# Seven products for eight in the up-projections of three feed-forward layers

## The chip, the core and the metric

The kernel runs on one core of a Trainium2 chip. The metric is the device time of one execution in microseconds (us), lower is better. Engines are named as in the profile: PE (TensorE, matrix products), DVE (VectorE), ACT (ScalarE), POOL (GpSimd), SP (here only an issuer of transfers).

## What is computed

Two blocks act on 512 tokens of 1024 features in float32. The first has two layers, each a mixer (a gated linear recurrence, then a sparse attention) and a convolutional feed-forward layer; the second has a gated feed-forward layer, a hybrid mixer and another gated feed-forward layer. The change is in the last three feed-forward layers: the convolutional one behind the attention, and both of the second block.

```
def swiglu(x, w_gu, w_down):                 # D_FF = 2816
    g, u = jnp.split(x @ w_gu, 2, axis=-1)   # w_gu [1024, 5632]
    return (jax.nn.silu(g) * u) @ w_down     # w_down [2816, 1024]

def conv_ffn(h, w_up, conv_w, conv_b, w_down):
    a, v = jnp.split(h @ w_up, 2, axis=-1)
    a = causal_conv3(a, conv_w) + conv_b     # along the tokens, per feature
    return (jax.nn.silu(a) * v) @ w_down
```

## The kernel before, in words

The residual `x` stays in SBUF, features on partitions. Every float32 operand of a large product is split into two float32r parts, h = round(a) on ACT (L186, L315) and l = a - h on DVE (L187, L318), and a product is three matmuls: h h, h l and l h (`fm`, L249, lines L274, L275, L277; `tm`, L284, with tokens on the output's partitions). Each matmul has a 128x128 weight tile of its own and up to 512 tokens.

All weights pass through one stream in the order of use. A block is 1024 rows (8 k tiles) by 256 columns; `w_dma` (L161) loads it on SP's queue into one of two raw buffers, `w_split` (L172) splits it in eight chunks of 512 elements per partition into one of three buffers for h and l, and `w_done` (L206) lets the next one start when a block has been used.

A feed-forward layer (`ffn`, L926) goes in three rounds, of 3, 4 and 4 groups. A group is 256 features: a block of the gate's columns and one of the value's columns, 96 matmuls of 512 tokens (the first group of a layer goes by token halves, 256 tokens, since its input is still being normalised). Gate tiles leave PSUM through `ev_a` (L937; silu, with the convolution also L950 and L952), value tiles through `ev_v` (L965; product L968 on DVE, then a split into the down projection's operand, L315 and L318). Then the round's part of the down projection is added to `x` (`out_proj`, L639; `resid`, L621, with L632); the last round's goes by token halves in its second half, and each half starts the next norm (`norm_half`, L394, with L376 and L388 or L390, and L428 where two norms follow each other). Squares for the norm are added up on POOL (L337).

The program order of each engine is the order in which the builder emits instructions. `Weave` (L64) counts the time of emitted matmuls, 0.000424 us per column, and lets side tasks (splits, norms, parts of mixers) emit their next step when their delay on that clock is over; `wait` runs a task to its end at once. PSUM has four banks for products (`pg`, L142) and four for side tasks (`pa`, L146).

Of the kernel before, what the change touches and what calls it, by code (L numbers as in the profile page):

```python
# [16 lines left out]
OP = mybir.AluOpType  # L17
# [10 lines left out]
RAW_BUFS, HL_BUFS, W2_BUFS = 2, 3, 10  # L28
# [24 lines left out]
class Tiles:  # L53
    """a [128, k, token] tile, with other tiles in place of its first ones."""
# [9 lines left out]
class Weave:  # L64
    """Interleaves side generators with the main stream, by emitted tensor-engine time (us)."""
# [13 lines left out]
    def _run(self, task):  # L79
        """one step; a generator yields the time to its next step, or None while it is blocked."""  # L80
        self.busy = True
        blocked = False
        try:
            dt = next(task.gen)
            blocked = dt is None
            self.n += 1
            heapq.heappush(self.q, (self.t + (0.3 if blocked else dt), self.n, task))
        except StopIteration:
            task.done = True
        self.busy = False  # L90
        return blocked
# [7 lines left out]
    def wait(self, task):  # L99
        """runs the task to its end, and others only while it is blocked."""  # L100
# [17 lines left out]
class Builder:  # L118
    def __init__(self, tc, I, out, ctx):
# [8 lines left out]
        self.nm = 0  # L128

# [21 lines left out]
    def w_init(self, blocks):  # L151
        self.wb = blocks
        self.w_dma_i = self.w_split_i = self.w_use_i = self.w_done_i = 0
        self.w_raw = {}
        self.w_hl = {}
        self.w_task = {}
        self.w_hold = False
        self.w_held = []
        self.gain = None

    def w_dma(self):  # L161
        i = self.w_dma_i
        if i >= len(self.wb):
            return
        self.w_dma_i += 1
        ap, r0, nk, c0, ncol = self.wb[i]
        raw = self.t([128, nk, ncol], "raw", RAW_BUFS)
        src = ap[r0 * 128:(r0 + nk) * 128, c0:c0 + ncol].rearrange("(k p) m -> p k m", p=128)
        self.nc.sync.dma_start(raw, src)
        self.w_raw[i] = raw  # L170

    def w_split(self, i, slow=True):  # L172
        nc = self.nc
        if i >= len(self.wb):
            return
        while i != self.w_split_i:
            yield None
        _, _, nk, _, ncol = self.wb[i]
        raw = self.w_raw.pop(i)
        h = self.t([128, nk, ncol], "wh", HL_BUFS, F32R)  # L180
        l = self.t([128, nk, ncol], "wl", HL_BUFS, F32R)
        self.w_hl[i] = (h, l)
        step = max(1, 512 // ncol)
        for k in range(0, nk, step):
            e = min(nk, k + step)
            nc.scalar.activation(h[:, k:e], raw[:, k:e], AF.Copy)  # L186
            nc.vector.tensor_tensor(l[:, k:e], raw[:, k:e], h[:, k:e].bitcast(F32), op=OP.subtract)  # L187
            if slow:
                yield MISC_D[0]
        self.w_split_i += 1  # L190
        self.w_dma()

    def w_start(self):
        self.w_dma()
        self.w_dma()
        for i in range(HL_BUFS):
            self.w_task[i] = self.wv.spawn(self.w_split(i), W2_D if i == 2 else 0.0)

    def w_get(self, want):
        i = self.w_use_i  # L200
        assert self.wb[i][1:] == want[1:] and str(self.wb[i][0]) == str(want[0]), (self.wb[i], want)
        self.w_use_i += 1
        self.wv.wait(self.w_task.pop(i))
        return self.w_hl.pop(i)

    def w_done(self, delay=0.7):  # L206
        i = self.w_done_i + HL_BUFS
        self.w_done_i += 1
        if i < len(self.wb):
            if self.w_hold:  # L210
                self.w_held.append(i)
            else:
                self.w_task[i] = self.wv.spawn(self.w_split(i), delay)
# [15 lines left out]
    def fm_merged(self, X, jobs, k_wait=None):  # L229
        """as fm, but with all of the jobs' features side by side in one loop over k; k_wait: (k, task) has  # L230
        the tiles from k on written by the task."""
# [4 lines left out]
        for k in range(nk):  # L236
            if k_wait is not None and k == k_wait[0]:
                self.wv.wait(k_wait[1])
            for j, m, p in todo:
                h, l = got[j]  # L240
                c = slice(m * 128, m * 128 + 128)
                self.mm3(p, h[:, k, c], l[:, k, c], xh[:, k, :], xl[:, k, :], k == 0, k == nk - 1)
# [3 lines left out]
        for _ in jobs:  # L246
            self.w_done()

    def fm(self, X, jobs, halves=False, kint=False, waits=(), last_delay=0.7):  # L249
        """jobs: list of (block, evac(mt_in_block, ps, lo, hi)); out[feature, token]."""  # L250
# [4 lines left out]
        for i, (lo, hi) in enumerate(parts):  # L255
# [3 lines left out]
            for jb, (b, ev) in enumerate(jobs):  # L259
                if jb not in got:  # L260
                    got[jb] = self.w_get(b)
                h, l = got[jb]
# [3 lines left out]
                for grp in groups:  # L266
                    pss = [self.pg() for _ in grp]
                    late = LATE if halves and kint and jb == 0 else 0
                    for k in range(nk + late):
                        for (m, mw), p in zip(grp, pss):  # L270
                            c = slice(m * 128, m * 128 + mw)
                            j = k - late
                            if k < nk:
                                mm(p[:mw, :n], h[:, k, c], xh[:, k, lo:hi], start=k == 0, stop=False)  # L274
                                mm(p[:mw, :n], l[:, k, c], xh[:, k, lo:hi], start=False, stop=False)  # L275
                            if j >= 0:
                                mm(p[:mw, :n], h[:, j, c], xl[:, j, lo:hi], start=False, stop=j == nk - 1)  # L277
# [3 lines left out]
                if i == len(parts) - 1:  # L281
                    self.w_done(last_delay if jb == len(jobs) - 1 else 0.7)

    def tm(self, X, jobs, halves=False, waits=()):  # L284
        """jobs: list of (block, evac(tok_tile, ps)); out[token, feature]."""
# [6 lines left out]
        for i, (j, t) in enumerate(order):  # L292
# [5 lines left out]
            h, l = got[j]  # L298
            nk, n = b[2], b[4]
            p = self.pg()  # L300
            for k in range(nk):
                tk = slice(t * 128, t * 128 + 128)
                mm = self.nc.tensor.matmul
                mm(p[:, :n], xh[:, k, tk], h[:, k, :], start=k == 0, stop=False)  # L304
                mm(p[:, :n], xh[:, k, tk], l[:, k, :], start=False, stop=False)  # L305
                mm(p[:, :n], xl[:, k, tk], h[:, k, :], start=False, stop=k == nk - 1)  # L306
                self.wv.pe(3 * n * 0.000424)
            ev(t, p)
            if t == 3:
                self.w_done()  # L310

    def split(self, h, l, src, engine="act"):
        """h + l = src, h and l float32r."""
# [7 lines left out]
    def norm_new(self, double=None):  # L321
        """squares of tiles below NPE are added up, the others go to the tensor engine one by one."""
# [24 lines left out]
    def rstd(self, ps, lo, hi):  # L347
        """[token, tile] reciprocal root of mean square + eps, from sums over 1024."""
# [8 lines left out]
    def bcast(self, ps, r, lo, hi):  # L357
        """ps[:, token] = r[token] on every partition."""
# [5 lines left out]
    def norm_outs(self, X, lo, hi, steps, ks=range(KT)):  # L364
        """X[k] = x[k] * gs[k] * ps (+ sh[k]) as float32r halves; steps(k): (gs, ps, sh)."""
# [28 lines left out]
    def norm_half(self, X, lo, hi, gs, sh=None, prev=None):  # L394
# [8 lines left out]
        if self.n_double is not None:  # L403
            # the second norm's mean square is the sum of (x g)^2 times the first's rstd^2
# [39 lines left out]
    def params(self):  # L444
        """Vectors over features, as columns: rows of 128 features are loaded and transposed."""
# [70 lines left out]
    def ada_cols(self, layer, j, acc, pai):  # L516
        """columns j*4 .. j*4+3 of the modulation, from partial sums over partitions."""
# [30 lines left out]
    def ada_first_load(self, js):  # L548
        """shift and scale of the first norm: 2048 columns, as four blocks in the big slots."""
# [7 lines left out]
    def ada_first_sums(self, j, pool=0):  # L557
        """sums over a block's row tiles, the first of them on the scalar engine and Pool."""
# [8 lines left out]
    def ada_first_mm(self, j):  # L567
        """a block's columns, as products on the tensor engine, each 128 times over."""
# [38 lines left out]
    def gs(self, name, layer, which):  # L607
        """norm gain times (1 + scale)."""
# [5 lines left out]
    def gs_part(self, t, name, layer, which, k0):  # L614
        """as gs, for four tiles of features."""
# [5 lines left out]
    def resid(self, first_mt, scale, norm):  # L621
        """evacuator: x[mt] += scale * ps."""
# [42 lines left out]
    def norm_to(self, gs, sh=None, double=None, tags=("hTh", "hTl")):  # L665
        """for out_proj's last blocks: a norm into a fresh X."""
# [8 lines left out]
    def next_norm(self, gs, sh=None, tags=("hTh", "hTl")):  # L675
        """starts a norm whose halves run as side tasks; returns (X, after_half)."""
# [9 lines left out]
    def hg_masks(self):  # L686
        """mask[m][s, t]: s in the first, t in the second half of the same block of 2m; mask[0]: s == t."""
# [23 lines left out]
    def hg_core(self, pair, v, o, B, done, gated, gain):  # L711
        """two heads: o[head] = rms-normed output of the gated recurrence, without its gain."""
# [62 lines left out]
        # s["T"]: [128, 4] chunk decays; q and k now carry the decay from and to the chunk's ends  # L775
# [140 lines left out]
    ROUNDS = ((0, 6), (6, 14), (14, 22))  # L916

    def ffn_blocks(self, up, down):
        out = []
        for a, b in self.ROUNDS:  # L920
            for t in range(a, b, 2):
                out += [(up, 0, 8, t * 128, 256), (up, 0, 8, DFF + t * 128, 256)]
# [3 lines left out]
    def ffn(self, X, waits, up, down, scale, after, conv=None):  # L926
        """x += scale * (act(X up_a) * (X up_v)) down; act: silu, or silu of the causal convolution."""
        nc = self.nc
        if conv is not None:
            cw, cb = conv  # L930
        for r, (a, b) in enumerate(self.ROUNDS):
            mh, ml = self.big("b0", F32R), self.big("b1", F32R)
            for t in range(a, b, 2):
# [36 lines left out]
                first = r == 0 and t == a  # L970
# [950 lines left out]
```

## Time and profile before

| | us |
|---|---|
| median of 3 runs (lowest, highest) | 2780.48 (2775.51, 2782.68) |
| span of the profiled execution, first to last instruction | 2771.8 |
| median less span | 8.7 |
| PE busy / PE weight loads busy | 2725.3 / 2309.7 |
| DVE busy / ACT busy / POOL busy | 1466.6 / 1052.3 / 280.1 |
| mean granted PE clock | 0.995 |

The page lists the span, and for the profiled execution no time of its own beside it. Matmuls overlap in the pipeline, so one matmul's duration is longer than the distance to the next, and a PE that is always busy can still be slow: what a stage takes is read from the distances. "Busy" of another engine includes time in which a started instruction is held up.

### The profile page before, as it was taken

The page shows a single profiled execution, that of the slowest core. Times are in us where ns is not written, and L with a number is a line of the kernel's source. Part 1 is how long each engine was busy: PE and PEld are TensorE (multiplying, and loading weights), DVE is VectorE, ACT ScalarE, POOL GpSimd, SP SyncE. Part 2 cuts the span into 40 slices and gives each one's busy share as a digit, 9 for nine tenths or more (in the row PEclk, how much of TensorE's full clock was granted, in tenths as well). Part 3 has the DMA queues.
Part 4 walks back from the last instruction along what each step waited for, and adds up shares of the span by engine and source line. Part 5 has one row for each costly group of instructions (what it writes and reads, how often), then busy time and mean ns, then how long its engine had stood idle before and what let it go on. Part 6 is the DMA issues. An engine that isn't in the chain of part 4 may idle for free.

```text
span 2771.8 us, 36529 instructions
## 1 busy us (share of the span) xinstructions
PE 2725.3 (98%) x14561; PEld 2309.7 (83%) x14561; DVE 1466.6 (53%) x2791; ACT 1052.3 (38%) x2044; POOL 280.1 (10%) x404
## 2 busy tenths in 40 slices
PE   6999999999999999999999999999999999999999
PEld 5988898888978888888889888897878987988888
DVE  7866567767544896544446333353455235533333
ACT  3323343323323895433334232343256333422222
POOL 3111110000101792000011000010000000100001
PEclk9999999999999999999999999999999999999999
DMA  7542126555231001233222322323433233232221
GB/s 251 185 152 71 59 92 198 175 175 182 79 107 61 1 2 64 97 100 106 91 92 84 99 91 97 102 63 108 105 78 88 54 89 105 77 101 96 92 92 60
DMA packets 254183, 278.69 MB, mean 101 GB/s; under 512 B 12952, under 2 KB 228397, under 8 KB 254013
## 3 DMA queue, kind: packets, MB, share of 16 engines
q1 hardware_dynamic: 226283, 233.21, 27.0%
q10 hardware_dynamic: 27730, 43.14, 4.8%
q8 instruction: 115, 1.88, 0.3%
q14 instruction: 55, 0.45, 0.1%
HBM read 274.23 MB, written 2.10 MB: 100 GB/s over the span
## 4 chain that ended last, share of the span: by engine, by line
PE 92%; DVE 4%; ACT 1%; POOL 1%; issue 1%; ACTq 0%; DMA 0%; DVEq 0%; POOLq 0%
PE pg L274 26%; PE pg L275 26%; PE pg L277 26%; PE pa L733 2%; PE pg L306 1%; PE pg L304 1%; PE pg L305 1%; PE pa L1279 1%; DVE w L546 1%; PE pa L1322 1%; PE pa L360 1%; PE pg L1238 1%; PE pg L1237 1%; PE pa L1048 1%; PE pa L344 1%
## 5 line engine op out<-in xcount | busy, mean ns | idle before, releaser
L187 DVE TENSOR_TENSOR wl<-raw,wh 128x512 fp32r<-128x512 f32 x842 | 571.1, 711 | 426.6 <-ACT wh L186 425.0
L274 PE MATMUL pg<-b,wh 128*128 128x512 f32 (+1 forms) x1856 | 672.6, 363 | 1.0 <-DVE w L968 1.0
L275 PE MATMUL pg<-b,wl 128*128 128x512 f32 (+1 forms) x1856 | 667.2, 360 | 0.0
L274 PE MATMUL pg<-hTh,wh 128*128 128x512 f32 (+3 forms) x1672 | 638.4, 383 | 1.8 <-ACT hTh L315 1.2
L275 PE MATMUL pg<-hTh,wl 128*128 128x512 f32 (+3 forms) x1672 | 633.1, 380 | 0.7 <-DVE wl L187 0.7
L277 PE MATMUL pg<-hTl,wh 128*128 128x512 f32 (+3 forms) x1672 | 621.5, 376 | 0.0
L186 ACT ACTIVATE wh<-raw 128x512 fp32r<-128x512 f32 x842 | 477.6, 619 | 279.8 <-PE pg L277 173.4
L277 PE MATMUL pg<-b,wh 128*128 128x512 f32 (+1 forms) x1472 | 523.9, 358 | 0.0
L275 PEld LDWEIGHTS pg<-b,wl 128*128 128x128 f32 x1856 | 348.8, 188 | 56.4
L274 PEld LDWEIGHTS pg<-b,wh 128*128 128x128 f32 x1856 | 348.6, 188 | 56.5 <-DVE w L968 1.4
L274 PEld LDWEIGHTS pg<-hTh,wh 128*128 128x128 f32 (+2 forms) x1672 | 313.4, 187 | 72.5 <-issue 4.6
L277 PEld LDWEIGHTS pg<-hTl,wh 128*128 128x128 f32 (+2 forms) x1672 | 310.4, 188 | 66.8 <-DVE hTl L318 0.4
L275 PEld LDWEIGHTS pg<-hTh,wl 128*128 128x128 f32 (+2 forms) x1672 | 313.5, 187 | 60.0 <-DVE wl L187 1.1
L277 PEld LDWEIGHTS pg<-b,wh 128*128 128x128 f32 x1472 | 275.2, 188 | 42.9
L337 POOL TENSOR_TENSOR w<-w,w 128x256 f32<-128x256 f32 (+1 forms) x78 | 78.1, 1006 | 1797.6 <-ACT w L336 1797.1
L315 ACT ACTIVATE b<-w 128x512 fp32r<-128x512 f32 (+1 forms) x112 | 67.4, 602 | 380.2 <-DVE w L968 314.8
L277 PE MATMUL pg<-hTh,wh 128*128 128x512 f32 (+1 forms) x384 | 142.9, 378 | 0.0
L968 DVE TENSOR_TENSOR w<-w,pg 128x512 f32<-128x512 f32 (+1 forms) x96 | 61.5, 641 | 146.7 <-PE pg L277 146.2
L318 DVE TENSOR_TENSOR b<-w,b 128x512 fp32r<-128x512 f32 (+1 forms) x112 | 73.3, 654 | 74.8 <-ACT b L315 74.8
L546 DVE SCALAR_TENSOR_TENSOR w<-w,cact,w 128x512 f32<-128x512 f32 x140 | 106.4, 760 | 4.2 <-DMA w<-in_ada_w_dram 3.6
L952 DVE SCALAR_TENSOR_TENSOR w<-pg,PT,w 128x511 f32<-128x511 f32 (+1 forms) x96 | 67.6, 704 | 75.6 <-ACT w L950 73.9
L632 DVE SCALAR_TENSOR_TENSOR x<-pg,mod,x 128x512 f32<-128x512 f32 (+1 forms) x80 | 50.5, 640 | 95.7 <-PE pg L277 90.7
(378 smaller groups left out, 2898.0 us busy)
## 6 DMA issues: line engine op xcount, KB each, us to landing
raw<-in_ffn_w_up_dram SPq DMA_DIRECT2D x44, 1024.0 KB
raw<-in_ffn_w_gu_dram SPq DMA_DIRECT2D x44, 1024.0 KB
w<-in_ada_w_dram ACTq DMA_DIRECT2D x160, 256.0 KB
raw<-in_ffn_w_down_dram SPq DMA_DIRECT2D x32, 1024.0 KB
raw<-in_w_in_dram SPq DMA_DIRECT2D x32, 1024.0 KB
raw<-in_hg_w_in_dram SPq DMA_DIRECT2D x16, 1024.0 KB
raw<-in_ffn_w_down_dram SPq DMA_DIRECT2D x16, 768.0 KB
raw<-in_nsa_w_in_dram SPq DMA_DIRECT2D x10, 1024.0 KB
```

Of the source, the lines that this page charges most:

```text
L186: nc.scalar.activation(h[:, k:e], raw[:, k:e], AF.Copy)
L187: nc.vector.tensor_tensor(l[:, k:e], raw[:, k:e], h[:, k:e].bitcast(F32), op=OP.subtract)
L274: mm(p[:mw, :n], h[:, k, c], xh[:, k, lo:hi], start=k == 0, stop=False)
L275: mm(p[:mw, :n], l[:, k, c], xh[:, k, lo:hi], start=False, stop=False)
L277: mm(p[:mw, :n], h[:, j, c], xl[:, j, lo:hi], start=False, stop=j == nk - 1)
L315: self.nc.scalar.activation(h, src, AF.Copy)
L318: self.nc.vector.tensor_tensor(l, src, h.bitcast(F32), op=OP.subtract)
L337: nc.gpsimd.tensor_tensor(acc[0][:, lo:hi], acc[0][:, lo:hi], sq[:, lo:hi], op=OP.add)
L546: nc.vector.scalar_tensor_tensor(acc, w, self.cact[:, k:k + 1], acc, op0=OP.mult, op1=OP.add)
L733: mm(p[:, c, :n], s["k"][:, cc], q, start=True, stop=True)
L952: nc.vector.scalar_tensor_tensor(c[:, lo + d:hi], p[:, :n - d], w(j), c[:, lo + d:hi], op0=OP.mult, op1=OP.add)
L968: nc.vector.tensor_tensor(s_[:, lo:hi], s_[:, lo:hi], p[:, :hi - lo], op=OP.mult)
```

## The change

Each group but a layer's first is computed as a 2x2 block product with seven multiplications (Strassen's scheme in Winograd's form). The two blocks of a group, gate and value columns by upper and lower half of the rows, are the quarters A11, A12 (gate) and A21, A22 (value); the input's quarters are halves of the features by halves of the tokens. The seven products use A11, A12, A22 and the sums S1 to S4 of weights, and four quarters of the input and four sums of them, called T.

- Weights: half blocks (four k tiles, 512 KB) are loaded into six raw buffers and split into six buffers for h and l. For a fast group `w_sums` and `w_after` form the sums on POOL, in the raw buffer of A21 (S3) and in one buffer X (S1, S2 and S4 one after the other). A sum goes through the same split as a loaded piece, two chunks of 512.
- Input: `fast_inputs` adds h and l back together per k on POOL, forms the four sums on DVE and POOL and splits them, once per layer, as a side task behind the two halves of the norm.
- Products: `fm_fast` runs the seven products, each with 24 matmuls of 256 tokens, accumulating into three banks A, E and F; A changes between two banks from group to group.
- Evacuation: `fast_group` copies partial results out of the banks on ACT (A11, S1, S2), adds on DVE (A12, S3, S4) and multiplies (A22 on DVE, S4's on POOL). With the convolution, tiles are first put together to 512 tokens; its shifted multiply-adds then read SBUF only.

The other layers and mixers use the new stream of half blocks, with the products as before.

```diff
-RAW_BUFS, HL_BUFS, W2_BUFS = 2, 3, 10
+RAW_BUFS, HL_BUFS, W2_BUFS = 6, 6, 11
+SUM_D, CHUNK_D, T_D = 2.6, 1.2, 1.2
...
+    def w_sums(self):
+        if self.g_sums == len(self.groups) or self.g_sums > self.g_free:
             return
...
+        g["X"] = self.t([128, 4, 256], "wsum")
+        tt(g["X"], a21, a22, op=OP.add)
+        tt(a21, a11, a21, op=OP.subtract)
...
+    def w_after(self, p):
...
+        if k == "S1":
+            tt(g["X"], g["X"], raw(0), op=OP.subtract)
+            self.raw_free(g["load"])
+        elif k == "S2":
+            tt(g["X"], raw(3), g["X"], op=OP.subtract)
+        elif k == "S4":
+            self.g_free += 1
+            self.w_sums()
...
     def w_split(self, i, slow=True):
...
+        if p["kind"] in ("S2", "S4"):
+            yield SUM_D
...
             if slow:
-                yield MISC_D[0]
+                yield MISC_D[0] if p["kind"] == "raw" else CHUNK_D
         self.w_split_i += 1
-        self.w_dma()
+        self.w_after(p)
...
+    def fast_inputs(self, X, tags, first, second):
...
+            for k in range(4):
+                left.append(whole(k, 0, store[:, k * 512:k * 512 + 512] if k < 2 else self.w2()))
+                yield T_D
+            yield from self.wv.wait_in(second)
+            yield 0.5
+            for k in range(4):
+                r, q = whole(k, 256, self.w2()), left[k]
+                yield T_D
+                a, b = self.w2(), self.w2()
+                tt = nc.vector.tensor_tensor
+                tt(a[:, 0:256], r[:, 0:256], q[:, 0:256], op=OP.subtract)
+                nc.gpsimd.tensor_tensor(a[:, 256:512], r[:, 256:512], r[:, 0:256], op=OP.subtract)
+                tt(b[:, 0:256], r[:, 256:512], a[:, 0:256], op=OP.subtract)
+                tt(b[:, 256:512], q[:, 256:512], b[:, 0:256], op=OP.subtract)
+                for i, f in enumerate((a, b)):
+                    self.split(th[:, i * 4 + k, :], tl[:, i * 4 + k, :], f)
+                    yield T_D
...
+    def fm_fast(self, X, T, blocks, after):
...
+        steps = (("A11", x(0, 0), "A"), ("S1", t(0, 0), "E"), ("S2", t(4, 0), "A"), ("A12", x(4, 0), "F"),
+                 ("S3", t(0, 256), "A"), ("S4", x(4, 256), "E"), ("A22", t(4, 256), "A"))
...
+            for m in range(2):
+                o = banks[b][:, m * 256:m * 256 + 256]
+                c = slice(m * 128, m * 128 + 128)
+                for k in range(4):
+                    xh, xl = (u[:, k0 + k, lo:lo + 256] for u, k0, lo in (h_, l_))
+                    mm(o, h[:, k, c], xh, start=first and k == 0 and m == 0, stop=False, skip_group_check=True)
+                    mm(o, h[:, k, c], xl, start=False, stop=False, skip_group_check=True)
+                    mm(o, l[:, k, c], xh, start=False, stop=k == 3 and m == 1, skip_group_check=True)
+                    self.wv.pe(3 * 256 * 0.000424)
+            self.w_done((p,), 0.1)
+            after(name, banks)
...
+            def after(step, banks):
+                A, E, F = (banks.get(n) for n in "AEF")
+                if step == "A11":
+                    c["1"] = self.w2()
+                    nc.scalar.activation(c["1"], A, AF.Copy)
...
+                elif step == "A12":
+                    nc.vector.tensor_tensor(c["1"], c["1"], F, op=OP.add)
+                    nc.scalar.activation(c["1"], c["1"], AF.Silu)
+                elif step == "S3":
+                    nc.vector.tensor_tensor(c["5"], c["5"], A, op=OP.add)
+                elif step == "S4":
+                    nc.vector.tensor_tensor(c["2"], c["2"], E, op=OP.add)
+                    nc.scalar.activation(c["2"], c["2"], AF.Silu)
+                    nc.gpsimd.tensor_tensor(c["2"], c["2"], c["5"], op=OP.mult)
+                    pend.append(self.wv.spawn(late(256, c["2"]), 1.2))
+                else:
+                    nc.vector.tensor_tensor(c["1"], c["1"], A, op=OP.mult)
+                    pend.append(self.wv.spawn(late(0, c["1"])))
...
+                if fast and not first:
+                    self.wv.wait(t_task)
+                    fast_group(a, t)
+                    continue
```

## Rows read from the trace of the kernel before

**Rows 1.** The page's first part: the span, and PE's busy time, share and instructions.

```profile
span 2771.8 us, 36529 instructions
PE 2725.3 (98%) x14561; PEld 2309.7 (83%) x14561; DVE 1466.6 (53%) x2791; ACT 1052.3 (38%) x2044; POOL 280.1 (10%) x404
```

**Rows 2.** The page's chain that ended last, shares of the span by engine.

```profile
PE 92%; DVE 4%; ACT 1%; POOL 1%; issue 1%; ACTq 0%; DMA 0%; DVEq 0%; POOLq 0%
```

**Rows 3.** Windows (us from the start): busy us (instructions) per engine, granted clock, DMA share.

```profile
1126.00:1448.00 322.00, 322.00 (x1397) 261.65 (x1396) 150.67 (x229) 109.69 (x191) 5.96 (x4) 1.00 0.30 98
1499.00:1820.00 321.00, 321.00 (x1392) 260.54 (x1391) 116.86 (x180) 89.26 (x162) 2.60 (x2) 1.00 0.30 98
2415.00:2737.00 322.00, 322.00 (x1397) 261.30 (x1396) 119.21 (x184) 89.67 (x163) 2.83 (x2) 1.00 0.29 93
...
2626.40:2715.70 89.30, 89.30 (x385) 72.04 (x384) 30.39 (x47) 25.97 (x47) 0.00 (x0) 1.00 0.27 90
```

**Rows 4.** Windows of a token-half stage on PE, and timeline of PE (start, us, instruction).

```profile
2399.80:2415.40 15.60, 15.60 (x135) 1.00 0.20 62
...
1080.07 0.28 PE L275 MATMUL pg<-b,wl 128*128 128x256 f32 x1
...
1080.64 0.28 PE L274 MATMUL pg<-b,wh 128*128 128x256 f32 x1
```

**Rows 5.** Groups by line and shape: count, busy us, mean ns, idle before.

```profile
L187 DVE TENSOR_TENSOR wl<-raw,wh 128x512 fp32r<-128x512 f32 x840 | 570.3, 711 | 423.9 <-ACT wh L186 422.2
L952 DVE SCALAR_TENSOR_TENSOR w<-pg,PT,w 128x511 f32<-128x511 f32 x40 | 30.0, 749 | 66.3 <-ACT w L950 66.3
...
L337 POOL TENSOR_TENSOR w<-w,w 128x512 f32<-128x512 f32 x30 | 41.5, 1388 | 1672.2 <-ACT w L336 1671.6
...
L186 ACT ACTIVATE wh<-raw 128x512 fp32r<-128x512 f32 x840 | 476.7, 619 | 276.6 <-PE pg L277 173.4 <-issue 87.7 <-DMA raw<-in_w_in_dram 6.5
```

**Rows 6.** Timeline of POOL and of DVE where both work: start, us, instructions merged.

```profile
1817.70 1.29 POOL L337 TENSOR_TENSOR w<-w,w 128x512 f32<-128x512 f32 x1 [4.20 <-ACT w L336]
...
1818.12 1.43 DVE L187 TENSOR_TENSOR wl<-raw,wh 128x512 fp32r<-128x512 f32 x1 [1.22 <-ACT wh L186]
...
18.93 6.02 POOL L337 TENSOR_TENSOR w<-w,w 128x512 f32<-128x512 f32 x4
...
2383.74 0.74 POOL L337 TENSOR_TENSOR w<-w,w 128x256 f32<-128x256 f32 x1 [5.43 <-ACT w L336]
...
2383.95 2.83 DVE L376 SCALAR_TENSOR_TENSOR w<-x,PT,pa 128x256 f32<-128x256 f32 x7 [0.73 <-PE pa L360]
```

**Rows 7.** Timeline of DVE and PE around the first groups of the three layers.

```profile
1116.49 2.85 DVE L390 SCALAR_TENSOR_TENSOR hTh<-w,mod,b 128x256 fp32r<-128x256 f32 x7
...
1123.73 0.99 DVE L952 SCALAR_TENSOR_TENSOR w<-pg,PT,w 128x255 f32<-128x255 f32 x2
...
1126.39 0.40 PE L274 MATMUL pg<-b,wh 128*128 128x512 f32 x1
...
1492.10 3.21 DVE L428 SCALAR_TENSOR_TENSOR x<-x,PT,pa 128x256 f32<-128x256 f32 x8
...
1499.52 0.40 PE L274 MATMUL pg<-hTh,wh 128*128 128x512 f32 x1
...
2399.92 2.83 DVE L376 SCALAR_TENSOR_TENSOR w<-x,PT,pa 128x256 f32<-128x256 f32 x7 [1.59 <-PE pa L360]
...
2403.39 2.43 DVE L388 TENSOR_TENSOR hTl<-w,hTh 128x256 fp32r<-128x256 f32 x7
...
2408.40 1.90 DVE L187 TENSOR_TENSOR wl<-raw,wh 128x512 fp32r<-128x512 f32 x3
...
2415.62 0.40 PE L274 MATMUL pg<-hTh,wh 128*128 128x512 f32 x1
```

**Rows 8.** Windows at the kernel's start, all engines.

```profile
30.00:35.00 5.00, 1.40 (x11) 1.10 (x9) 3.93 (x8) 1.12 (x2) 0.00 (x0) 0.85 1.05 387
35.00:40.00 5.00, 4.57 (x10) 2.89 (x10) 5.00 (x9) 4.40 (x9) 0.00 (x0) 0.50 0.29 98
```

More of the change, by code (lines that the diff above doesn't have):

```diff
@@ new lines, in w_dma, with raw_free @@
+        self.w_sums()
+    def raw_free(self, i):
+        self.w_freed.add(i)
+        while self.w_free_to in self.w_freed:
+            self.w_free_to += 1
+        self.w_dma()
+    def w_sums(self):
+        if self.g_sums == len(self.groups) or self.g_sums > self.g_free:
+            return
+        g = self.groups[self.g_sums]
+        if g["load"] + 2 >= self.w_dma_i:
+            return
+        self.g_sums += 1
+        tt = self.nc.gpsimd.tensor_tensor
+        a11, a21, a22 = (self.w_raw[g["load"] + i] for i in range(3))
+        g["X"] = self.t([128, 4, 256], "wsum")
+        tt(g["X"], a21, a22, op=OP.add)
+        tt(a21, a11, a21, op=OP.subtract)
+        g["sums"] = True
@@ L172, in w_split @@
     def w_split(self, i, slow=True):
         nc = self.nc
-        if i >= len(self.wb):
-            return
         while i != self.w_split_i:
             yield None
[L178 to L181, printed above, removed]
+        p = self.pieces[i]
+        while p["kind"] != "raw" and p["kind"][0] == "S" and not p["g"]["sums"]:
+            yield None
+        if p["kind"] in ("S2", "S4"):
+            yield SUM_D
@@ L202, in w_get @@
         self.w_use_i += 1
[L203 to L213, printed above, removed]
+        ps = self.item_pieces[i]
+        if have[0] == "S":
+            return ps
+        for p in ps:
+            self.wv.wait(self.w_task.pop(p))
@@ L245, in fm_merged @@
             jobs[j][1](m, p, 0, S)
-        for _ in jobs:
-            self.w_done()
+        for at in got:
+            self.w_done(at.pieces)
     def fm(self, X, jobs, halves=False, kint=False, waits=(), last_delay=0.7):
@@ L309, in tm, with whole, run @@
             if t == 3:
-                self.w_done()
+                self.w_done(got[j].pieces)
+    def fast_inputs(self, X, tags, first, second):
+        nc = self.nc
+        xh, xl = X
+        th, tl = self.big(tags[0], F32R), self.big(tags[1], F32R)
+        two = lambda t: t.rearrange("p (i t) -> p i t", t=256)
+        def whole(k, lo, f):
+            nc.gpsimd.tensor_tensor(two(f), xh[:, k::4, lo:lo + 256].bitcast(F32), xl[:, k::4, lo:lo + 256].bitcast(F32),
+                                    op=OP.add)
+            return f
+        def run():
+            yield from self.wv.wait_in(first)
+            yield 1.5
+            left = []
+            store = self.t([128, 1024], "hmask")
+            for k in range(4):
[15 more added lines that the diff above has]
+                    yield T_D
+        return (th, tl), self.wv.spawn(run())
@@ new lines, in fm_fast @@
+    def fm_fast(self, X, T, blocks, after):
+        mm = self.nc.tensor.matmul
+        x = lambda k0, lo: tuple((t, k0, lo) for t in X)
+        t = lambda k0, lo: tuple((u, k0, lo) for u in T)
+        steps = (("A11", x(0, 0), "A"), ("S1", t(0, 0), "E"), ("S2", t(4, 0), "A"), ("A12", x(4, 0), "F"),
+                 ("S3", t(0, 256), "A"), ("S4", x(4, 256), "E"), ("A22", t(4, 256), "A"))
+        self.fast_banks = self.fast_banks or [self.pg() for _ in range(4)]
+        self.fast_banks[:2] = self.fast_banks[1::-1]
+        place = dict(zip("AEF", self.fast_banks[1:]))
+        banks = {}
+        for p, (name, (h_, l_), b) in zip(self.w_get(*blocks), steps):
+            assert self.pieces[p]["kind"] == name
+            h, l = self.w_piece(p)
+            first = b not in banks
+            if first:
+                banks[b] = place[b]
+            for m in range(2):
[9 more added lines that the diff above has]
+            after(name, banks)
@@ L916, with ffn_blocks @@
     ROUNDS = ((0, 6), (6, 14), (14, 22))
-    def ffn_blocks(self, up, down):
+    def ffn_blocks(self, up, down, fast=False):
         out = []
```

214 lines of the change are left out of this document (165 added, 49 removed).

## Prediction, made before the change was run

> **What bounds the kernel now.** I read the page first. TensorE is busy for 2725 of the 2771.8 us span [rows 1], and the chain that ended last lies on it for 92% [rows 2], so time is gained only by giving TensorE less to stream, and only while the other engines keep up. Then the windows of the three feed-forward layers behind their first group: 322, 321 and 322 us each, TensorE busy throughout at the full granted clock of 1.00, VectorE busy for 151, 117 and 119 us, GpSimd for 6 or less [rows 3]. Four up-projection groups without convolution take 89.3 us [rows 3], 22.33 us each. A group is two weight blocks of 256 columns: 96 matmuls of 512 tokens, so 0.2326 us a matmul. The page gives the span, not the profiled execution's whole time; the median of the runs is 2780.5 us, 8.7 us above the span, and I count from 2780.5 with those 8.7 us unchanged.
>
> **What is removed.** In ten of eleven groups of each of three layers, 30 groups, eight quarter products become seven. Each is 24 matmuls (two column tiles, four k, three high/low terms) of 256 tokens, so a group has 168. The price of a 256-token matmul, its own weight load included, is in the trace: the token-half stage shows 135 records touching 15.60 us, two or three of them across its ends, 0.118 us each; elsewhere five follow each other in 0.57 us, 0.114 [rows 4]. Both are near half of 0.2326. I take 0.1178, because that stretch multiplies the same kind of tile as the change does. A product is then 2.83 us, a group 19.8 us, and the saving 2.54 us a group, **76 us** in all. At 0.114 a group is 19.15 us and the saving 95 us.
>
> **What is added, per group.** The factors to be split are seven of 1024 elements per partition where there were four: 14 splits by ScalarE and VectorE instead of 8. GpSimd, idle in these rounds, gets four sums of 1024 columns and a product of 512 (two of 256 with the convolution). Evacuation on VectorE becomes three adds and a product from PSUM and two late splits.
> - ScalarE: 21 operations without the convolution, 23 with it, about 0.62 us each [rows 5]: 13.0 to 14.3 us of 19.8. It is covered.
> - VectorE: three 512-wide splits in a row take 1.90 us, seven halves in a row 2.43 us [rows 7]: 0.63 and 0.35 us each with the last one's tail, so I take 0.605 and 0.335 in a long row. Sixteen splits are 9.7 us and four operations on PSUM 2.4: 12.1 us. With the convolution come four shifted multiply-adds whose two tensors now both lie in SBUF (0.75 us alone [rows 5], about 0.665 in a row), and its evacuations are halves: 15.0 us.
> - GpSimd: 0.74 us for 256 columns and 1.29 for 512 where it starts first [rows 6], so 0.55 per further 256 and an estimated 2.4 us for 1024; bounds are twice the 512's 1.1 and twice its 1.388 mean [rows 5]. In all 11 us of 19.8.
>
> **The two do not simply overlap.** A split that VectorE starts 0.42 us into a 1.29 us GpSimd add takes 1.43 us, where the mean of 840 is 0.71 [rows 5], and ends 0.56 us behind the add. At the start of the kernel four adds take 6.02 us, 1.5 each, beside VectorE's multiply-adds. Operations with one tensor in PSUM are not slowed: seven of them, the first two beside an add, take 2.83 us [rows 6], the same as seven with no add near [rows 7]. So a 512-wide add takes about 1.1 us out of VectorE's stream of splits, a 256-wide one 0.55 and a 1024-wide one 2.2. The Trainium skill, SBUF — State Buffer, section "Who interferes with whom", says why: a VectorE instruction with two SBUF inputs and a GpSimd instruction that reads SBUF exclude each other for the whole instruction, and PSUM inputs are exempt. The trace agrees at 256 and 512 columns; no row shows 1024. By that rule the sum keeps its two lock terms (12 and 6 us, below); were a long add shared instead, they would be zero and the sum 2731 us.
>
> The four sums and the product hold 4 x 2.2 + 1.1 = 9.9 us. Packed into one group, VectorE's stream is 12.1 + 9.9 = 22.0 us, with the convolution 24.9 us, both over TensorE's 19.8. But the builder spreads them. A piece's two chunks are emitted 1.2 us apart and S2 and S4 wait 2.6 more: 14 x 1.2 + 2 x 2.6 = 22.0 us on a clock that counts 18.2 us for a group, so about 23.9 us of real time. The six pieces of lookahead fall by about one and a half per group and last a round of four, which the down projection then refills. The 14 splits and four sums of a group thus cost 0.83 of their price within its time: 7.0 + 7.3, with 1.2 for late splits, 1.1 for the product and 2.4 on PSUM, 19.0 us, under 19.8; with the convolution 21.9 us, of which 2.6 on PSUM may run beside an add, so 19.3 to 21.9. I take 1.2 us over in each of ten convolution groups, **12 us** (0 to 25), and 0.3 us in each of the other twenty, **6 us** (0 to 30): VectorE at 95% is sometimes late for S3's add, behind which TensorE has only one product, 2.83 us, before it needs the bank.
>
> **The first fast group of a layer.** S1 needs sums of the input's quarters. Per k these are two whole adds on GpSimd (the first done early), a half subtraction there, three halves and two splits on VectorE: behind the second token half 1.1 + 0.55 + 1.0 + 1.2 = 3.86 us, four times 15.4. In the last layer VectorE is free of the norm at 2405.8; with 2.7 us of evacuation and a 1.2 us weight split the sums are there at 2425.1. TensorE reaches group 1 at 2415.6 and S1's fourth k 3.9 us later, at 2419.5: a wait of 5.6 us. In the layer before, VectorE comes free at 1495.3, behind eight updates of the doubled norm and with half of the evacuation done, and group 1 starts at 1499.5 [rows 7]: 9.9 us. In the convolutional layer it is free at 1119.3, evacuates for 5.5 us more (twice 0.99 for a tile's shifted multiply-adds among it), and TensorE is there at 1126.4 [rows 7]: 11.1 us. Together **27 us**. If GpSimd runs further ahead, a third of that, 9; if splits for S2 and A12 come first and the clock falls, 45. Where TensorE was busy for 1.40 of 5 us the granted clock next stood at 0.50 of full, the 1.2 GHz level [rows 8], which over a 5 us window costs 2.5 us.
>
> **Edits at no cost.** Loads of 512 KB twice as often: DMA is at 0.30 in these stages [rows 3]; if a load were late, the next split would. At the start three megabytes of weights go ahead of the second modulation blocks instead of two; DMA is at 1.05 until 35 us and at 0.29 behind it, moving 387 GB/s [rows 8], so the landing slips by 2.7 us, to some 38 us. VectorE is busy for all of 35 to 40 us [rows 8] with work that comes first; without that cover it costs 3 us. The last late split of a round is hidden by the down projection's first seven k, 9.8 us.
>
> **Sum.** 2780.5 - 76 + 27 + 12 + 6 = 2749 us.
>
> **Rivals.**
> - *The forecast*, part given back: 2749, between 2725 and 2772. Chance 0.45.
> - *TensorE paces everything*: the VectorE terms vanish and the first group costs 9 us: 2780.5 - 76 + 9 = 2713 us (2694 at the shorter matmul). For it speaks VectorE's idle share of over half now [rows 3]; against it the 1.43 us split [rows 6]. Chance 0.20.
> - *VectorE with GpSimd becomes the bound*, the other sign: place, the steady groups; price, 22.0 and 24.9 us a group. Twenty groups save 0.33 each and ten lose 2.57, with 27 us in front: 2780.5 - 6.6 + 25.7 + 27 = 2827 us; with half of the PSUM work beside the adds, 20.8 and 23.6 us a group, 2790. It decides where VectorE falls more than 2.83 us behind S3's add or behind the copy of A, so that TensorE stops in each product. For it: adds and multiply-adds that hold each other up [rows 6]. Against: the spread emission. Chance 0.20.
> - *Gain and loss cancel*: first groups at 45 us and steady groups at 20.6 and 22.2 us give 2780.5 - 34.6 - 1.3 + 45 = 2790; with the first groups at 27, 2772. Between them lies no change. Chance 0.15.
>
> **Numbers.** A measurement of this kernel tells about 0.3%, 8.3 us, from no change: faster is below 2772, slower above 2789. Faster holds the first two cases, 0.65; within 0.3% the last, 0.15; slower the third, 0.20. The range leaves out a tenth on either side: 2710 takes in the undisturbed case at the usual matmul, 2800 the milder end of the VectorE bound.
>
> **What would show it.** Right: up-projection windows of the two plain layers near 80 us per four groups with TensorE busy; 256-token matmuls at 0.118 us; GpSimd adds near 2.4 us, with splits stretched to 2 us or more beside them; waits of 6 to 11 us at S1 of the first fast group, for VectorE. Wrong: four groups over 86 us, matmuls of the A bank waiting for VectorE in each product (the third rival); no wait at S1 (the second); or a start or attention stage that is several us longer, which I count at nothing.

## The result and the profile after

The kernel became slower: 2952.5 us (median of four, 2948.1 to 2955.9) against 2781.1 us, a ratio of 1.0625 [1.0608, 1.0641]. The forecast was 2749 us, range 2710 to 2800.

The profile's page after the change, to be read beside [rows 1]:

```profile
span 2946.4 us, 42499 instructions
PE 2727.4 (93%) x16721; PEld 2400.9 (81%) x16721; DVE 1823.2 (62%) x3139; ACT 1214.4 (41%) x2356; POOL 681.6 (23%) x600
```

PE is busy as long as before, in 174.6 us more, so it now stands idle. VectorE is busy for 357 us more and still idle for 38% of the span. The windows of the fast rounds show where (us from the start; busy and instructions of PE, PEld, DVE, ACT, POOL; granted clock; DMA share and GB/s). The first three are the convolutional layer's, with 2, 4 and 4 fast groups, the others those of the second block's first layer:

```profile
1125.80:1193.50 67.70, 46.97 (x336) 43.87 (x336) 51.12 (x69) 27.12 (x49) 22.55 (x12) 0.82 0.16 51
1234.20:1351.70 117.50, 90.84 (x673) 85.88 (x671) 74.30 (x99) 46.81 (x83) 38.78 (x19) 0.91 0.23 72
1402.40:1515.30 112.90, 90.61 (x673) 87.17 (x671) 71.02 (x95) 43.48 (x77) 35.51 (x18) 0.91 0.21 66
1603.30:1663.80 60.50, 45.51 (x337) 43.00 (x337) 44.57 (x55) 25.17 (x48) 23.99 (x13) 0.86 0.18 58
1697.10:1797.10 100.00, 86.11 (x674) 80.91 (x673) 65.93 (x75) 43.84 (x80) 40.89 (x17) 1.00 0.27 85
1841.50:1937.40 95.90, 84.37 (x674) 80.42 (x672) 64.52 (x71) 40.73 (x74) 36.33 (x16) 1.00 0.24 78
```

Four groups took 89.3 us before [rows 3]; now 96 to 118. The distance between matmuls that don't wait is the forecast 0.118 us (e5 below: 674 in 79.66 us), so the loss is in gaps and, in the rounds with the longest ones, in a lower granted clock (0.82 to 0.91) as well. What PE waits for (line, releaser and its line, total us, times, longest):

```profile
PE pg L475 <- ACT wh L267: 53.1, 24, 5.7
PE pg L477 <- DVE wl L268: 53.1, 102, 1.8
PE pg L475 <- ACT b L485: 16.0, 5, 4.2
...
PE pg L476 <- DVE b L488: 9.3, 9, 3.9
...
PE pg L475 <- ACT hTl L485: 8.6, 3, 3.5
```

L267 and L268 split weight pieces; L485 and L488 split the input's sums. So the weight pieces come late, a hundred times by a little. One such wait, S2's in a plain group, in the timeline (start, us; in brackets the idle time before, and what ended it):

```profile
1750.62 2.41 POOL L240 TENSOR_TENSOR wsum<-wsum,raw 128x1024 f32<-128x1024 f32 x1 [4.06 <-DVE wl L268]
...
1752.79 0.60 ACT L1124 ACTIVATE w<-pg 128x512 f32<-128x512 f32 x1 [2.56 <-PE pg L477]
...
1753.28 1.14 ACT L267 ACTIVATE wh<-wsum 128x512 fp32r<-128x512 f32 x2
...
1753.94 1.29 DVE L268 TENSOR_TENSOR wl<-wsum,wh 128x512 fp32r<-128x512 f32 x2 [3.39 <-ACT wh L267]
...
1753.96 0.39 PE L475 MATMUL pg<-b,wh 128*128 128x256 f32 x1 [1.21 <-ACT wh L267]
...
1261.12 0.58 PE L475 MATMUL pg<-b,wh 128*128 128x256 f32 x1 [5.67 <-ACT wh L267]
```

ScalarE had been idle for 2.56 us, yet S2's split stands in its queue behind L1124, the copy of the result of S1, the product just ahead of S2. It was issued only when S2 was needed, so PE waits for copy and split. The copy is only the last of two here: the sum that the split reads (L240) ended at 1753.03, 0.25 us before the split began. But in e2 below, which has no sums, this wait is the same 1.20 us. In a convolutional group (last line) A11's split stands behind the convolution's whole chain, 5.67 us. Counted in the order in which the program issues splits and products: when it comes to 132 of the 210 fast products, not even their own piece has been split to the end; a round opens with 2 or 4 pieces ahead, not 6, and loses about 2 per group.

### The profile page after: what moved, and what is told of

Read it like the earlier page. It is cut to its first block, busy times and chain, and to the rows that moved or that the text cites. A ratio compares the mean times of both kernels' runs of the same rounds, so it can differ in the third digit from the quotient of the medians.

```text
span 2946.4 us, 42499 instructions
## 1 busy us (share of the span) xinstructions
PE 2727.4 (93%) x16721; PEld 2400.9 (81%) x16721; DVE 1823.2 (62%) x3139; ACT 1214.4 (41%) x2356; POOL 681.6 (23%) x600
## 5 line engine op out<-in xcount | busy, mean ns | idle before, releaser
L268 DVE TENSOR_TENSOR wl<-raw,wh 128x512 fp32r<-128x512 f32 (+1 forms) x860 | 717.0, 867 | 289.0 <-ACT wh L267 286.2
L267 ACT ACTIVATE wh<-raw 128x512 fp32r<-128x512 f32 (+1 forms) x860 | 480.4, 610 | 153.9 <-PE pg L378 123.3
L375 PE MATMUL pg<-hTh,wh 128*128 128x512 f32 (+2 forms) x1032 | 384.4, 374 | 1.7 <-ACT hTh L485 1.2
L376 PE MATMUL pg<-hTh,wl 128*128 128x512 f32 (+2 forms) x1032 | 378.9, 369 | 0.7 <-DVE wl L268 0.5
L378 PE MATMUL pg<-hTl,wh 128*128 128x512 f32 (+2 forms) x1032 | 370.1, 366 | 0.0
L375 PEld LDWEIGHTS pg<-b,wh 128*128 128x128 f32 x1536 | 290.1, 189 | 57.0 <-ACT wh L267 13.9
L475 PE MATMUL pg<-b,wh 128*128 128x256 f32 x880 | 257.0, 292 | 66.4 <-ACT wh L267 45.6
L378 PEld LDWEIGHTS pg<-b,wh 128*128 128x128 f32 x1472 | 276.7, 189 | 43.3
L476 PE MATMUL pg<-b,wh 128*128 128x256 f32 x960 | 274.3, 286 | 9.3 <-DVE b L488 9.3
L477 PE MATMUL pg<-b,wl 128*128 128x256 f32 x880 | 259.0, 294 | 20.4 <-DVE wl L268 20.2
L475 PEld LDWEIGHTS pg<-b,wh 128*128 128x128 f32 x880 | 173.3, 197 | 72.4 <-ACT wh L267 51.2
L375 PEld LDWEIGHTS pg<-hTh,wh 128*128 128x128 f32 (+1 forms) x1032 | 192.7, 187 | 42.6 <-issue 4.6
L376 PEld LDWEIGHTS pg<-hTh,wl 128*128 128x128 f32 (+1 forms) x1032 | 192.7, 187 | 32.7 <-DVE wl L268 1.1
L476 PEld LDWEIGHTS pg<-b,wh 128*128 128x128 f32 x960 | 185.3, 193 | 11.7 <-DVE b L488 11.7
L268 DVE TENSOR_TENSOR wl<-wsum,wh 128x512 fp32r<-128x512 f32 x180 | 122.3, 704 | 104.4 <-ACT wh L267 103.9
```

What stands on the lines that cost most here:

```text
L267: nc.scalar.activation(h[:, k:e, :ncol], src[:, k:e, :ncol], AF.Copy)
L268: nc.vector.tensor_tensor(l[:, k:e, :ncol], src[:, k:e, :ncol], h[:, k:e, :ncol].bitcast(F32), op=OP.subtract)
L375: mm(p[:mw, :n], h[:, c], xh[:, k, lo:hi], start=k == 0, stop=False)
L376: mm(p[:mw, :n], l[:, c], xh[:, k, lo:hi], start=False, stop=False)
L378: mm(p[:mw, :n], at(j)[0][:, c], xl[:, j, lo:hi], start=False, stop=j == nk - 1)
L475: mm(o, h[:, k, c], xh, start=first and k == 0 and m == 0, stop=False, skip_group_check=True)
```

## Experiments

Each is a variant of the changed kernel, compared with before on the same chip; times are medians. Before's own median lay between 2775 and 2781 us in these comparisons, so differences between variants that ran apart are good to about 6 us. A gap is PE's idle time, as in the brackets of a timeline. My first theory: the pause between a piece's splits makes the program issue them too slowly. Rivals: VectorE and GpSimd excluding each other; the sums of the input; the new stream.

**e1: the pause.**

```diff
-SUM_D, CHUNK_D, T_D = 2.6, 1.2, 1.2
+SUM_D, CHUNK_D, T_D = 2.6, 0.6, 1.2
```

> Only the pause that the program order leaves between a weight piece's two splits is halved (1.2 to 0.6), so that a group's splits take 14 x 0.6 + 2 x 2.6 = 13.6 us on the clock that orders the work, instead of 22.0, against the 18.2 us that its products count. Theory (the splits are issued slower than the products use them, so each stands directly ahead of its own product): the 5 to 8 us of gaps in each fast group mostly go, the four-group rounds fall from 96 to 118 us to 80 to 95, and the kernel to 2790 to 2860 us. Rival (VectorE and GpSimd excluding each other, or the sums' one buffer, set the pace): same work, same pace, 2935 to 2965 us.

2894.9 us, 1.0424 [1.0409, 1.0440]: 58 us back, outside what either expected. All 210 products now have 3 to 5 pieces ahead, and no fast product waits for a weight piece any more. Another wait has come:

```profile
PE pg L475 <- ACT w L1121: 73.8, 21, 6.4
PE pg L475 <- ACT b L485: 21.0, 5, 5.8
PE pg L475 <- DVE w L1134: 10.5, 8, 1.4
PE pg L475 <- ACT hTl L485: 9.8, 3, 5.5
...
PE pg L476 <- DVE b L488: 8.1, 9, 1.6
```

L1121 copies A11's result out of the bank that S2 writes. The timeline leads back from one gap:

```profile
1706.08 3.49 DVE L268 TENSOR_TENSOR wl<-raw,wh 128x512 fp32r<-128x512 f32 x2
1709.50 0.67 DVE L1134 TENSOR_TENSOR w<-w,pg 128x512 f32<-128x512 f32 x1
...
1706.30 2.73 POOL L243 TENSOR_TENSOR wsum<-raw,wsum 128x1024 f32<-128x1024 f32 x1 [2.13 <-issue]
...
1710.20 0.63 ACT L1135 ACTIVATE w<-w 128x512 f32<-128x512 f32 x1 [3.81 <-DVE w L1134]
...
1714.59 0.63 ACT L485 ACTIVATE b<-w 128x512 fp32r<-128x512 f32 x1 [1.72 <-DVE w L1139]
1715.12 0.58 ACT L1121 ACTIVATE w<-pg 128x512 f32<-128x512 f32 x1
...
1715.75 0.38 PE L475 MATMUL pg<-b,wh 128*128 128x256 f32 x1 [2.22 <-ACT w L1121]
```

A split beside GpSimd's 2.73 us addition holds VectorE (3.49 us for two); the addition L1134 stands behind it; ScalarE stands 3.81 us at the Silu that reads it, then at a late split; the copy that PE needs is behind both. So there is a second cause, which the first had partly covered. The first rounds of four, of the convolutional layer and of the second block's first:

```profile
1229.28:1335.48 106.20, 87.62 (x673) 86.75 (x672) 80.18 (x103) 47.34 (x84) 36.39 (x19) 0.89 0.29 90
1662.00:1755.60 93.60, 85.30 (x674) 84.48 (x673) 71.58 (x79) 43.90 (x81) 37.23 (x17) 0.95 0.33 102
```

**e2: no sums, long pause.** `w_sums` and `w_after` issue no additions; S1 to S4 are split from raw tiles.

```diff
-        tt(g["X"], a21, a22, op=OP.add)
-        tt(a21, a11, a21, op=OP.subtract)
...
-            tt(g["X"], g["X"], raw(0), op=OP.subtract)
...
-            tt(g["X"], raw(3), g["X"], op=OP.subtract)
```

> GpSimd's four additions on the weights of each group are left out (the pieces S1 to S4 are split straight from loaded tiles, so the products are of other factors); the pace of issue stays. Theory (pace of issue): only the part of the gaps that waits for a sum goes, about 1.4 us ahead of S2 and of S4 each, some 2 to 3 us of the 5 to 8 per group: 2870 to 2915 us. Rival (the sums and their lock on VectorE set the pace): most gaps go, under 2840 us.

2877.1 us, 1.0359 [1.0343, 1.0374], as the pace theory expected. Pieces still come late:

```profile
PE pg L469 <- ACT wh L261: 44.5, 23, 4.4
PE pg L471 <- DVE wl L262: 29.4, 48, 1.1
```

**e3: the convolutional layer in the old way**, in `blocks` and `build`:

```diff
-        out += self.ffn_blocks(I["ffn_w_up"][1], I["ffn_w_down"][1], True)
+        out += self.ffn_blocks(I["ffn_w_up"][1], I["ffn_w_down"][1])
...
-        self.conv_ffn(st["X"], st["tasks"], 1, begin2, ("hTl", "b3"))
+        self.conv_ffn(st["X"], st["tasks"], 1, begin2)
```

> The convolutional layer is computed in the old way, the two others stay changed. The theory puts 75 us of the loss into this layer's rounds and 8 into its down projections, so 2865 to 2880 us; the 5.95 us gap ahead of A11's first product in each convolutional group, behind the convolution's ScalarE work, goes with it. Rival (the loss lies in what the three layers share): a third of it goes, 2893 to 2900 us.

2849.2 us, 1.0256 [1.0239, 1.0273]. The loss of this layer is 103 us, more than I had put on it; the other two lose 38 each against e4. From its second group to the next layer's first fast group, this kernel's windows:

```profile
1126.30:1448.30 322.00, 322.00 (x1396) 261.62 (x1395) 150.38 (x234) 110.63 (x194) 6.02 (x4) 1.00 0.32 99
1448.30:1504.60 56.30, 51.57 (x433) 50.79 (x431) 40.65 (x87) 26.67 (x60) 27.10 (x23) 1.00 0.15 47
```

Together 378.3 us; the changed kernel takes from 1125.8 to 1603.3 for the same, 477.5 us.

**e4: all three layers in the old way on the new stream**, e3's edit for each.

> All three layers in the old way, on the new stream of half blocks with six buffers of each kind: no sums, no new products, no input sums. Theory (the stream costs nothing): 2770 to 2790 us. Rival (the new stream costs part of the loss by its order of loads and splits): over 2800 us.

2773.1 us, 0.9985 [0.9976, 0.9995]: the stream costs nothing.

**e5: e1 and e2 together.**

> Both earlier edits at once: the shorter pause and no sums on GpSimd (products of other factors). In the run with the shorter pause alone one gap a group is left, ahead of S2's first matmul, 2.6 us in the plain and 5.5 in the convolutional layer, with 1.5 us at the half clock behind it: S2 waits for ScalarE's copy of A11's result, which stands behind two Silus that wait for VectorE additions, which stand behind splits of 2.9 us beside a 1024-wide GpSimd addition. Theory (late issue and the sums' hold on VectorE are the two causes, one after the other): nothing is left but the input sums, four-group rounds of the plain layers 80 to 82 us, kernel 2775 to 2800 us. Rival (the order of ScalarE's queue alone makes the gap): 2850 us or more.

2767.5 us, 0.9966 [0.9954, 0.9977], better than expected. Four plain groups, then four convolutional ones:

```profile
1602.50:1682.16 79.66, 79.66 (x674) 79.65 (x673) 51.74 (x78) 44.08 (x80) 5.18 (x4) 1.00 0.38 119
...
1217.84:1308.86 91.02, 84.67 (x673) 84.06 (x672) 60.10 (x102) 47.59 (x84) 4.43 (x6) 0.94 0.34 104
```

The first is 19.9 us a group with PE never idle, the forecast's 19.8. The sums cost 75 us with the long pause and 127 with the short one: they matter more where late issue no longer hides them. Leaving out the sums alone gives back 75 us, shortening the pause alone 58, both 185: neither is the whole cause.

The convolutional groups are not clean even so. Besides the input's sums, PE waits for the copy of A11 (here L1115), which stands in ScalarE's queue behind the convolution's Silu (L1154) and the late splits:

```profile
PE pg L469 <- ACT w L1115: 14.8, 7, 2.1
PE pg L469 <- ACT b L479: 13.0, 4, 3.5
...
PE pg L469 <- ACT hTl L479: 6.5, 2, 3.5
PE pg L470 <- DVE b L482: 4.2, 9, 1.0
...
1241.14 0.63 ACT L1154 ACTIVATE w<-w 128x512 f32<-128x512 f32 x1 [1.66 <-DVE w L1153]
```

**e6: e1, and Silus and the convolution's chain issued later** (`gate`, `late` and `chain` are side tasks).

```diff
-                    nc.scalar.activation(c["1"], c["1"], AF.Silu)
+                    c["t"] = self.wv.spawn(gate(c["1"]), 1.5)
...
-                    nc.scalar.activation(c["2"], c["2"], AF.Silu)
-                    nc.gpsimd.tensor_tensor(c["2"], c["2"], c["5"], op=OP.mult)
-                    pend.append(self.wv.spawn(late(256, c["2"]), 1.2))
+                    pend.append(self.wv.spawn(late(256, c["2"], c["5"]), 1.5))
```

> Shorter pause, sums in place, and the Silus and the convolution's chain are issued 1.5 us later on the ordering clock, behind other ScalarE work, so that ScalarE's queue does not stand at them while VectorE is behind. Theory (the gap ahead of S2 is handed on through ScalarE's queue): it shrinks to under 1 us, 2800 to 2850 us. Rival (VectorE beside the sums is too slow whatever stands in ScalarE's queue): 2880 to 2910 us.

2834.2 us, 1.0210 [1.0193, 1.0227]. The wait for A11's copy (now L1129) falls from 73.8 to 28.7 us; in plain groups the gap ahead of S2 is 0.5 us or less, in convolutional ones still 2.5 to 3.5:

```profile
PE pg L475 <- ACT w L1129: 28.7, 21, 3.5
PE pg L475 <- ACT b L485: 20.5, 5, 5.8
PE pg L475 <- DVE w L1142: 17.7, 14, 1.4
```

**e7: e1, and each 1024-wide addition as two of 512.**

```diff
-        tt(g["X"], a21, a22, op=OP.add)
+        for k in (0, 2):
+            tt(g["X"][:, k:k + 2], a21[:, k:k + 2], a22[:, k:k + 2], op=OP.add)
```

> Shorter pause, and each of the four 1024-wide GpSimd additions of a group is made as two of 512 columns: the same work, but VectorE gets in between. Theory (how long one addition keeps VectorE out decides): a split or an evacuation waits some 1.3 us less, the gap ahead of S2 falls from 2.6 to about 1 us or goes, 2835 to 2870 us. Rival (what decides is how long the two exclude each other in all): 2885 to 2905 us.

2873.9 us, 1.0351 [1.0335, 1.0366], between the two: 21 us from e1. S2's gap in the plain groups, 2.2 to 2.5 us in e1, falls only to 1.5 to 2.5. A half takes 1.49 to 1.64 us on average, two of them 3.0 to 3.3, where a whole one takes 2.44 to 2.66 in the changed kernel. Shorter holds help, but GpSimd is then busy longer in all (736 us against 680 in e1; VectorE's busy time is the same within 4 us); how much of the rest that makes up this run doesn't settle.

**e8: e1 without the input's sums.**

```diff
-            T, t_task = self.fast_inputs(X, tags, *waits)
+            T = X
...
-                    self.wv.wait(t_task)
```

> Shorter pause; the sums of the input's blocks and their splits are left out, the products read the input's own tiles in their place (other factors, the same matmuls). In the run with the shorter pause the first fast group of each layer stands 17.5, 18.2 and 15.8 us longer than its matmuls need. Theory (that is the wait for the input sums and the clock lost behind it): 51 us go, 2838 to 2850 us. Rival (the first group would wait for its late weight pieces just as long): 2875 us or more.

2849.3 us, 1.0260 [1.0244, 1.0276]: the input's sums cost 45.6 us against e1.

**e12: e6's later issue with the long pause.**

> Only the Silus and the convolution's chain are issued later; the long pause stays. Theory (with the long pause the plain layers' gaps wait for pieces that are issued just ahead of their products, not for ScalarE's copies of results): the plain layers' four-group rounds stay within 4 us of 100 and 96; in the convolutional layer the 6 us gap ahead of A11, behind the chain in ScalarE's queue, falls by half or more in most of its groups; kernel 2895 to 2940 us. Rival (what stands in ScalarE's queue is the whole cause, and the pause only shifts it): 2850 us or less.

2897.1 us, 1.0435 [1.0417, 1.0452]: the plain rounds hardly move, the convolutional ones fall from 117.5 and 112.9 to 108.3 and 99.5 us.

```profile
1234.70:1343.00 108.30, 91.02 (x674) 85.45 (x673) 76.07 (x100) 48.32 (x86) 39.76 (x19) 0.95 0.25 78
...
1663.00:1762.30 99.30, 85.93 (x674) 80.80 (x673) 69.97 (x76) 43.69 (x81) 40.91 (x17) 1.00 0.27 85
```

In a plain round of four, then, later Silus alone give 1 to 3 us, the short pause alone 2 to 7, both 10 to 14: each cause stands behind the other.

**e9 to e11: a version that beats both kernels.** e6 and e7 together, the convolutional layer in the old way, and the first round of the two plain layers in the old way, so that the input's sums are ready in time:

```diff
-                out += [("S", *pair)] if fast and t else pair
+                out += [("S", *pair)] if fast and a else pair
...
-                if fast and not first:
+                if fast and r:
```

> A version that should beat both kernels: the convolutional layer in the old way; in the two plain layers the first round in the old way, so that the input sums are ready before the first fast group; shorter pause, Silus issued later, sums as additions of 512 columns. Theory (late issue, sums against VectorE, and input sums were the three losses): 16 fast groups at 20.3 to 21.3 us instead of 22.3, no gap at the input sums, 2745 to 2765 us. Rival (a fast group costs elsewhere what it saves): 2770 us or more.

2752.6 us, 0.9913 [0.9900, 0.9926]: faster than before by 23 us, which is under 1% but clear of the interval.

```profile
span 2750.9 us, 40213 instructions
PE 2692.4 (98%) x15713; PEld 2341.0 (85%) x15713; DVE 1666.5 (61%) x2977; ACT 1143.2 (42%) x2222; POOL 532.7 (19%) x572
```

The first of its four fast rounds among its windows:

```profile
1578.46:1662.43 83.97, 81.22 (x674) 80.06 (x673) 70.04 (x78) 43.88 (x81) 44.19 (x28) 1.00 0.37 114
```

Four groups take 84.0 us, 21.0 each. Sixteen of them save 16 x (22.33 - 21.0) = 21 us, which with e4's 4 is about what was measured.

With the convolutional layer's last two rounds new as well:

> As the run with two layers, and the convolutional layer too has its last two rounds in the new way, with its chain issued step by step later. Theory: its groups, 24.3 us in the run with the later Silus, come to 23 to 24 us, more than the 22.3 of the old way, so this is 5 to 15 us slower than the run with two layers: 2755 to 2775 us. Rival (smaller additions free VectorE enough for the convolution too): equal or faster, under 2750 us.

2770.0 us, 0.9980 [0.9970, 0.9990], 17 us behind e9: its groups take 23.7 us, more than the old way's 22.33.

With S3's sum behind A11's subtraction:

> As the run with two layers, but S3's sum is made after A11 has been taken from the common sum, not ahead of it, so that S2's chain is two additions of 512 shorter. Theory: S2's and S1's remaining gaps shrink or stay, 0 to 8 us faster than the run with two layers. Rival (order among GpSimd's additions is indifferent): within 3 us of it.

2753.5 us, 0.9924 [0.9911, 0.9937], no different from e9. The gap of 0.4 to 0.7 us ahead of S1 went, the one ahead of S2 grew from 0.4 to between 1.2 and 1.7.

## Why the prediction was wrong, step by step

- **Products.** Right for the plain layers: e5 shows 19.9 us a group with nothing in the way. In the convolutional layer no run shows the saving: four groups take 91.0 us even in e5, and in the old way 89.4 (the kernel before):

```profile
1288.00:1377.40 89.40, 89.40 (x389) 72.84 (x388) 37.55 (x57) 25.70 (x45) 0.00 (x0) 1.00 0.29 94
```

- **Stream, loads, start.** Right: nothing (e4).
- **The lookahead.** This is the step that failed first: "The six pieces of lookahead fall by about one and a half per group and last a round of four, which the down projection then refills." I had the pace, 22.0 us of issue against 18.2 us of products, and read it as a relief for VectorE ("the builder spreads them"). But the six buffers are not six pieces in hand. The last pieces are let go only when the down projection's last block has been used, so a round opens with 2 or 4; about 2 go per group; in most rounds the first or second group uses up the last one. From there each piece is issued when its product asks for it, and latencies that I had taken as covered, copy, split, convolution chain, lie on PE's path. The shorter pause alone gives back 58 us (e1), and behind it a second loss shows.
- **VectorE and GpSimd.** This step failed too. The mechanism was right, its size not: 18 us were put on it. A 2.73 us addition stretches the split beside it to 2.9 us (e1: 3.49 us for two, of which one alone takes about 0.6). The Trainium skill, SBUF — State Buffer, section "Who interferes with whom", has such a pair exclude each other for the whole instruction; the trace now agrees at 1024 columns too. What I left out is the way on: VectorE's delay stops ScalarE's queue at a Silu, and the copy behind that Silu stops PE. I had set ScalarE at "covered" by its busy time, 13 to 14 us of 19.8. With the short pause, the sums are worth 127 us (e1 to e5; 75 with the pause in place, e2), and issuing the Silus and the chain later, with the sums in place, gives 61 back (e1 to e6).
- **The first fast group.** 27 us forecast, bounds 9 and 45; measured 45.6 (e8 against e1). Most of it is waiting, not the clock that the upper bound names: PE's waits for the input's sums come to 33.9 us in the changed kernel (16.0, 9.3 and 8.6 above) and to 38.9 in e1 (21.0, 9.8 and 8.1). The forecast left out that GpSimd's additions for the weights fall among VectorE's subtractions for the input. One of these, 0.42 us where nothing is beside it, takes 2.52:

```profile
1604.10 2.53 POOL L240 TENSOR_TENSOR wsum<-wsum,raw 128x1024 f32<-128x1024 f32 x1 [7.76 <-DVE wl L268]
...
1604.40 2.52 DVE L446 TENSOR_TENSOR w<-w,w 128x256 f32<-128x256 f32 x1
```

Without these additions (e5) the waits come to 23.7 us (13.0, 6.5 and 4.2). The clock adds to them. In the second block's first layer PE waits 12.5 us in all (9.9 forecast) at S1, and the granted clock is 0.50, the 1.2 GHz level, from the second of these windows on, still in the fourth, where PE works for 4.14 of 5 us:

```profile
1606.00:1611.00 5.00, 1.96 (x10) 0.84 0.32 105
1611.00:1616.00 5.00, 0.58 (x1) 0.50 0.00 0
1616.00:1621.00 5.00, 0.79 (x2) 0.50 0.00 0
1621.00:1626.00 5.00, 4.14 (x17) 0.50 0.08 16
```

- **The convolution.** Its groups were forecast at 1.2 us over 19.8; they took 29 to 33 where the lookahead was gone. The chain is long in latency, not in busy time, and stood in ScalarE's queue ahead of A11's split (e12, e3). With neither late issue nor sums (e5) they still take 22.8 us on average, as the chain then delays the copy of A11; the granted clock there is 0.94.
- **The rivals.** The third had the sign, but not the place: VectorE is busy for 66 of 100 us in the plain rounds, so it isn't the bound, and PE waits for pieces. With the short pause (e1) that rival comes near: PE waits at the copy of A, which it names, and a group takes 23.4 us, with the convolution 26.6, where it has 22.0 and 24.9; yet VectorE is busy for only 71.6 of 93.6 us. Against it I had held "the spread emission", which caused the first part of the loss. 2952 us lies beyond every case because none let PE wait for issue itself as well.

## What to carry to other kernels

Where a builder orders the work by its own clock, find how many pieces are really issued ahead when a stage begins and how many go per round; at zero, every latency of a producer lies on the consumer's path, however idle the engines are. An engine with in-order queues isn't covered because its busy time is small: list what stands ahead of each copy that frees a bank, and what that waits for. And when one wait is removed, look at the chain behind it before counting the gain: here two causes hid each other.

## What the runs showed of the hardware

Splitting GpSimd's additions made them dearer where VectorE comes between: 1.49 to 1.64 us for 512 columns on average (e7), where the shortest take 1.25 to 1.29. In the changed kernel's plain rounds of four, with gaps of 0.7 to 1.8 us, the granted clock was 1.00; in e1's, with 2.2 to 2.5 us ahead of each S2 but the first, 0.95 (behind the gap that ends at 1715.75 it stands at 0.50, and matmuls follow each other at 0.21 us in place of 0.118 from 1716.5 to 1719.7, some 1.5 us more); in the convolutional rounds of four, with gaps of 4.6 to 5.7 us, 0.91 over the whole round.
